# Order of the first loads in a one-core decoder trunk: cache pages ahead of the x tiles, and two more key groups in the opening

## The chip, the cores and the metric

The kernel runs on one core of one Trainium2 chip. The metric is the device time of one execution in microseconds (us), the median over the runs shown. The core has five engines that work side by side and wait for each other by semaphores: TensorE (PE in the profile, its weight loads PEld), VectorE (DVE), ScalarE (ACT), GpSimd (POOL) and SyncE (SP), which here issues nearly all DMAs. On each of them instructions run in the order in which they were queued.

## The reference

The program is one inference step of a two-layer decoder trunk with D = 1024, run for a prompt of 16 meta tokens and 1024 tokens and for 8 samples of 4 new tokens each. Only what this change touches is cut out here:

```
# layer 0, first module
h  = rms_norm(x, norm_mix[0])                  # over all tokens
a, g = split(h @ w_pw1 + b_pw1, 2)
u  = a * sigmoid(g)
y  = causal_dwconv(u, width 31) + b_dw
x  = x + silu(layer_norm(y)) @ w_pw2 + b_pw2
...
# layer 1, sample attention over the paged cache: 8 samples x 16 pages of 128 keys
for phys in page_table:                        # 128 pages in all
    c = cache_kv_latent[phys]                  # (128 keys, 128)
    k = rms_norm(einsum('pc,chd->phd', c, w_uk))   # 16 heads of 64, norm over d
    ...
```

The norm of each cached key does not depend on the tokens. The kernel therefore works out the sums of squares of all 128 x 128 x 16 key vectors during layer 0, long before the attention needs them.

## The kernel before

**Layout.** Activations are kept transposed: 8 tiles x0 to x7 of 128 channels by 1074 token columns (`T0`), 550 KB each. Every float32 operand of a matmul is split into a high part (`ch`, `xh`, `wh`, an ACT copy to fp32r) and a low part (`cl`, `xl`, `wl`, a subtraction on DVE or POOL), and a product is three matmuls: high x high, high x low, low x high. `split` (line 132) does it.

**Key groups.** `cache_norms` (line 634) is a generator that yields 256 times. Each step is one key group: for one page and one half of the 16 heads, three 128x512 matmuls into a PSUM tile `pk` (line 654), an ACT square (line 658, or on some places eight squares with accumulation, line 669) and a sum over each head (a DVE reduction, line 665, in some places after halvings on POOL, line 663). The generator fetches pages four at a time: `fetch(g)` (line 637) loads four latent pages of 128x128 values into one tile `ct` and splits it; `fetch(g + 1)` comes when the third group of page set g is due. There are two `ct`, `ch` and `cl` tiles each and two `pk` tiles.

**Where the groups are called.** `groups(n)` takes the next n steps. The places are fixed numbers: `FIRST0` = 16 ahead of the norm of x and `FIRST` = 30 behind it, both within the opening in which TensorE's order is left to the planner; then 24 for each of the channel blocks c = 1 to 7 (one behind every sixth matmul of the gate gemm of line 419); 12 and 1 and 4 around the last convolution and the layer norm; 8 in the first two column blocks of the `pw2` product (one behind every 18th matmul) and then one behind every ninth matmul, until the 256 are used up. Whatever is taken earlier is missing there: the list runs dry earlier.

**Opening.** `conv_phase` (line 334) loads the key weights `wuk`, the page table `pt` and then the x tiles. `page_table` (line 599) clamps the table on DVE, and `pages` (line 604) lets SP read four page numbers from it into registers and issue one DMA for each page. The SP order in this part is written out by hand: `more(XFIRST)` issues that many tiles of the list x0, ..., x7, `c1` (the constants), and after each page load `between`, a copy of `XPAT`, says how many tiles follow. Before the change this gives:

```
x0 x1 x2 | p0 - p1 x3 p2 - p3 x4 | p4 x5 p5 x6 p6 x7 p7 c1 | weights pw1
```

The sums of squares of x (`sq_add`, line 276: an ACT square and a DVE addition for each tile) lead by `add_rows` (line 295), `rows_rstd` (line 303) and `spread` (line 263) to the norm factor `rstd`. Line 370 scales each x tile with it on DVE, `split` makes `xh` and `xl`, and the first gemm (`gemms`, line 165, matmuls on line 175) of block c = 0 takes them one k after the other. Its two results go through a sigmoid and a product (`glu`, line 397), while TensorE has only key groups to do. Then blocks c = 1 to 7 follow, each with a 31-tap convolution on DVE (line 523) beside the next block's gemm.

**What decides the order.** Instructions on TensorE inside a `manual` block and SP's loads inside `manual_schedule` keep the order of the program. All others are ordered at build time by a planner that simulates the program and prefers higher priorities (`PRIO` = 2000 for the norm of x and for its splits, `PRIO3` = 0 for the first 16 groups).

Of the kernel before, what the change touches and what calls it, by code (L numbers as in the profile page):

```python
# [32 lines left out]
REST = 0  # L33
EVERY2 = 9
EVERY3 = 18
FIRST = 30
FILL0 = 1
FILL2 = 4
NLN = 0
# [21 lines left out]
FILLQ = 4  # L61
ND = 512
FIRST0 = 16
XFIRST = 3
ONPL3 = (1, 3, 5, 7)
PRIO3 = 0
XORD = (0, 1, 2, 3, 4, 5, 6, 7, 8)
XPAT = (0, 1, 0, 1, 1, 1, 1, 1)
ONPL = (0, 2, 4, 6)
ONPL0 = (1, 4, 7)  # L70
PEFILL = (1, 11)
# [47 lines left out]
class Prog:  # L119
# [214 lines left out]
    def conv_phase(self):  # L334
# [3 lines left out]
        with ExitStack() as es:  # L338
# [5 lines left out]
            todo = [(self.c1, a["c1"]) if k == KD else (xs[k], a["x0"][k]) for k in XORD]  # L344
            self.between = list(XPAT)

            def more(n):
                for _ in range(n):
                    nc.sync.dma_start(*todo.pop(0))
            self.more = more  # L350
            with self.tc.manual_schedule(engines={nc.sync.engine}):
                more(XFIRST)
            self.on_dve, self.on_pool = range(8), ONPL3
# [25 lines left out]
            self.on_dve, self.on_pool = range(8), ONPL2  # L379
            self.groups(FIRST)  # L380
            ws = [self.weight(a["pw1"][j * 8], 1024) for j in range(2)]
# [252 lines left out]
    def cache_norms(self):  # L634
        nc, a, kp, ss = self.nc, self.a, self.kp, self.ss

        def fetch(g):
            ct = kp.tile([128, 4, 128], F32, name="ct")
            self.pages(self.pt, 4 * g, [(ct, lambda p: a["ctn"][p].rearrange("a p n -> p (a n)")[:, 0:128])])
            ch, cl = kp.tile([128, 4, 128], F32R, name="ch"), kp.tile([128, 4, 128], F32R, name="cl")  # L640
            self.split(ch, cl, ct, eng=nc.gpsimd if self.help else None)
            return ch, cl

        nxt = fetch(0)
        for g in range(32):
            ch, cl = nxt
            for j in range(4):
                p = 4 * g + j
                for c in range(2):
                    if j == 1 and c == 0 and g < 31:  # L650
                        nxt = fetch(g + 1)
                    ps = self.pk.tile([128, 512], F32, name="pk")
                    for i, (s, m) in enumerate(((ch, self.ukh), (cl, self.ukh), (ch, self.ukl))):
                        x = nc.tensor.matmul(ps, s[:, j, :], m[:, 512 * c:512 * c + 512], start=i == 0, stop=i == 2)  # L654
                    self.pks.append(x)
                    if 2 * j + c in self.on_dve or 2 * j + c in self.on_pool:
                        q = self.ks.tile([128, 512], F32, name="sq")
                        nc.scalar.activation(q, ps, AF.Square)  # L658
                        v, n = q.rearrange("p (a b) -> p a b", b=64), 64
                        while 2 * j + c in self.on_pool and n > self.halve:  # L660
                            n //= 2
                            to = v[:, :, :n] if n > 1 else ss[:, p, 8 * c:8 * c + 8].rearrange("p (a b) -> p a b", b=1)
                            nc.gpsimd.tensor_tensor(out=to, in0=v[:, :, :n], in1=v[:, :, n:2 * n], op=ALU.add)  # L663
                        if n > 1:
                            nc.vector.tensor_reduce(out=ss[:, p, 8 * c:8 * c + 8], in_=v[:, :, :n], op=ALU.add, axis=AX.X)
                    else:
                        for h in range(8):
                            q = kp.tile([128, 64], F32, name="qq")
                            nc.scalar.activation(q, ps[:, 64 * h:64 * h + 64], AF.Square, accum_out=ss[:, p, 8 * c + h:8 * c + h + 1])  # L669
                    yield  # L670
# [1223 lines left out]
```

## Time and profile before

| what | value |
|---|---|
| runs of the kernel before | 2760.22, 2759.51, 2752.87 us, median 2759.51 |
| profiled execution, its own time | 2764.96 us |
| span of its instructions | 2763.0 us |
| busy share of the span | PE 96%, PEld 89%, DVE 68%, ACT 49%, POOL 26% |
| mean granted clock of TensorE | 0.98 |
| moved by DMA | 238.24 MB, mean 86 GB/s |

The profile is of one execution. Its times run from the first instruction; 2.0 us of the execution's own time lie around the span. An engine is busy when an instruction is on it; a matmul's end is modelled, so the distance from one matmul's start to the next says more of its cost than its duration does. "x<-y" is an instruction that writes tile x from y, and a wait is put down to the engine and line that ended it.

### The profile page before, as it was taken

The page shows a single profiled execution, that of the slowest core. Times are in us where ns is not written, and L with a number is a line of the kernel's source. Part 1 is how long each engine was busy: PE and PEld are TensorE (multiplying, and loading weights), DVE is VectorE, ACT ScalarE, POOL GpSimd, SP SyncE. Part 2 cuts the span into 40 slices and gives each one's busy share as a digit, 9 for nine tenths or more (in the row PEclk, how much of TensorE's full clock was granted, in tenths as well). Part 3 has the DMA queues.
Part 4 walks back from the last instruction along what each step waited for, and adds up shares of the span by engine and source line. Part 5 has one row for each costly group of instructions (what it writes and reads, how often), then busy time and mean ns, then how long its engine had stood idle before and what let it go on. Part 6 is the DMA issues. An engine that isn't in the chain of part 4 may idle for free.

```text
span 2763.0 us, 46569 instructions
## 1 busy us (share of the span) xinstructions
PE 2654.5 (96%) x16966; PEld 2449.1 (89%) x16966; DVE 1879.3 (68%) x3485; ACT 1356.8 (49%) x3701; POOL 709.8 (26%) x1019
## 2 busy tenths in 40 slices
PE   7999998999999999999889999999999999999999
PEld 6888876999999999999767776667999999999999
DVE  8899986578888875145677777676378777775232
ACT  6777775345544553023555555576245454453010
POOL 1567663023332330001111212120023333330000
PEclk9999997999999999999889999999999999999999
DMA  4111101502222236132100001367302222226122
GB/s 142 56 41 55 39 28 43 175 30 92 90 92 91 79 120 229 41 95 92 37 10 19 24 24 32 90 202 261 140 24 90 80 80 81 80 96 244 41 87 76
DMA packets 127770, 238.24 MB, mean 86 GB/s; under 512 B 39779, under 2 KB 81141, under 8 KB 127413
## 3 DMA queue, kind: packets, MB, share of 16 engines
q1 hardware_dynamic: 103828, 200.82, 22.4%
q0 software_dynamic: 9600, 32.36, 3.1%
q10 hardware_dynamic: 14112, 2.09, 0.5%
q8 instruction: 133, 2.18, 0.3%
q14 instruction: 97, 0.79, 0.1%
HBM read 183.90 MB, written 51.31 MB: 85 GB/s over the span
## 4 chain that ended last, share of the span: by engine, by line
PE 84%; DVE 6%; ACT 5%; DMA 2%; issue 2%; SPq 0%; POOL 0%; ACTq 0%; DVEq 0%; POOLq 0%
PE ps L797 29%; PE ps L175 22%; PE pk L654 5%; PE g L419 4%; PE v L1339 4%; PE ps L846 3%; PE p L151 2%; PE ps L197 2%; PE ps L1015 1%; PE p L1349 1%; PE p L1351 1%; PE p L1352 1%; PE po L1653 1%; PE s L1309 1%; PE ps L151 1%
## 5 line engine op out<-in xcount | busy, mean ns | idle before, releaser
L135 ACT ACTIVATE wh<-raw 128x512 fp32r<-128x512 f32 (+2 forms) x256 | 191.1, 749 | 539.7 <-PE ps L175 338.2
L136 DVE TENSOR_TENSOR wl<-raw,wh 128x512 fp32r<-128x512 f32 (+2 forms) x244 | 201.5, 829 | 107.4 <-ACT wh L135 105.1
L944 DVE TENSOR_TENSOR x<-ps,x 128x1074 f32<-128x1074 f32 (+1 forms) x48 | 61.0, 1270 | 291.5 <-PE ps L175 291.3
L767 DVE SCALAR_TENSOR_TENSOR c<-ub,c,c 128x1040 f32<-128x1040 f32 (+1 forms) x176 | 225.3, 1312 | 29.5 <-ACT c L763 28.4
L669 ACT ACTIVATE qq<-pk 128x64 f32<-128x64 f32 x736 | 158.4, 244 | 67.8 <-PE pk L654 67.7
L761 POOL COPY sb<-ub 128x32 f32<-128x32 f32 x88 | 87.6, 997 | 393.3 <-DVE ub L808 353.1
L1339 PE MATMUL v<-pf,vf 128*128 128x512 f32 (+4 forms) x448 | 174.4, 473 | 11.1 <-ACT pf L1356 10.7
L663 POOL TENSOR_TENSOR sq<-sq 128x256 f32<-128x256 f32 (+4 forms) x229 | 140.1, 620 | 102.1 <-ACT sq L658 95.1
L1356 ACT ACTIVATE pf<-p 128x512 f32<-128x512 f32 (+4 forms) x224 | 99.1, 450 | 118.0 <-DVE p L1354 97.4
L175 PE MATMUL ps<-xh,wh 128*128 128x358 f32 (+1 forms) x672 | 148.1, 329 | 9.2 <-ACT xh L135 5.9
L669 ACT ACTIVATION_READ_ACCUMULATOR qq<-pk 128x1 f32 x736 | 154.2, 228 | 0.0
L523 DVE SCALAR_TENSOR_TENSOR a<-u,c,a 128x512 f32<-128x512 f32 x216 | 150.2, 747 | 4.9 <-ACT a L516 4.9
L175 PE MATMUL ps<-xl,wh 128*128 128x358 f32 (+1 forms) x672 | 147.8, 328 | 0.1
L175 PE MATMUL ps<-xh,wl 128*128 128x358 f32 (+1 forms) x672 | 147.3, 327 | 0.0
L175 PE MATMUL ps<-al,wh 128*128 128x358 f32 (+1 forms) x672 | 147.2, 327 | 0.0
L175 PE MATMUL ps<-ah,wl 128*128 128x358 f32 (+1 forms) x672 | 146.5, 326 | 0.0
L175 PE MATMUL ps<-ah,wh 128*128 128x358 f32 (+1 forms) x672 | 146.2, 326 | 0.0
L654 PE MATMUL pk<-ukh,ch 128*128 128x512 f32 x256 | 115.3, 451 | 26.1 <-ACT ch L135 13.6
L763 ACT ACTIVATE c<-ub,c 128x1074 f32<-128x1074 f32 (+1 forms) x88 | 101.5, 1187 | 60.0 <-DVE ub L808 46.3
L175 PEld LDWEIGHTS ps<-xh,wh 128*128 128x128 f32 x672 | 117.2, 191 | 12.8 <-ACT xh L135 6.8
L658 ACT ACTIVATE sq<-pk 128x512 f32<-128x512 f32 x164 | 99.8, 613 | 50.3 <-PE pk L654 47.5
L135 ACT ACTIVATE wh<-s 128x512 fp32r<-128x512 f32 x120 | 75.6, 630 | 93.5 <-PE ps L797 86.7
(599 smaller groups left out, 9111.5 us busy)
## 6 DMA issues: line engine op xcount, KB each, us to landing
raw<-wup SPq DMA_DIRECT2D x88, 512.0 KB, 3.6
pg<-ctn SPq DMA_DIRECT2D x128, 192.0 KB, 3.8
raw<-wdn SPq DMA_DIRECT2D x32, 448.0 KB, 3.4
raw<-pw SPq DMA_DIRECT2D x24, 512.0 KB, 3.9
d_a<-c POOLq DMA_DIRECT2D x22, 537.0 KB, 3.5
raw<-d_a SPq DMA_DIRECT2D x22, 537.0 KB, 5.1
d_a<-c POOLq DMA_DIRECT2D x22, 531.0 KB, 3.2
raw<-d_a SPq DMA_DIRECT2D x22, 531.0 KB, 5.3
```

Source lines behind the costliest of these rows:

```text
L135: return (nc.scalar.activation(h, src, AF.Copy), (eng or nc.vector).tensor_tensor(out=l, in0=src, in1=h.bitcast(F32), op=ALU.subtract))
L136: (eng or nc.vector).tensor_tensor(out=l, in0=src, in1=h.bitcast(F32), op=ALU.subtract))
L175: nc.tensor.matmul(p[:, c, :ch], s[:, k * 128:(k + 1) * 128], m[k][:, off + c * ch:off + (c + 1) * ch], start=k == 0 and i == 0, stop=k == ...
L419: y = nc.tensor.matmul(p[:, 0], x[:, k * 128:(k + 1) * 128], m[k][:, t * ch:t * ch + ch], start=k == 0 and i == 0, stop=k == KD - 1 and i ...
L523: nc.vector.scalar_tensor_tensor(out=p[:, :ND] if j == n - 1 else acc, in0=x[:, j:j + ND], scalar=w[:, j:j + 1], in1=to if j == 1 else acc ...
L654: x = nc.tensor.matmul(ps, s[:, j, :], m[:, 512 * c:512 * c + 512], start=i == 0, stop=i == 2)
L663: nc.gpsimd.tensor_tensor(out=to, in0=v[:, :, :n], in1=v[:, :, n:2 * n], op=ALU.add)
L669: nc.scalar.activation(q, ps[:, 64 * h:64 * h + 64], AF.Square, accum_out=ss[:, p, 8 * c + h:8 * c + h + 1])
L763: x = nc.scalar.activation(c, ub, AF.Copy, scale=wd[:, t, 2:3])
L767: nc.vector.scalar_tensor_tensor(out=c[:, 2:pe], in0=ub[:, tap:tap + pe - 2], scalar=wd[:, t, tap:tap + 1], in1=c[:, 2:pe], op0=ALU.mult, ...
L797: nc.tensor.matmul(ps, w[:, s], m[:, lo:hi], start=first and k == 0 and i == 0, stop=k == KD // 2 - 1 and i == 2, skip_group_check=True)
L1339: nc.tensor.matmul(o[:, at_:], vf[:m, b, c], p[:m, :512 - at_], start=b == 0, stop=last)
```

## The change

Three numbers and one branch change. `XFIRST` goes from 3 to 0 and `XPAT` from (0, 1, 0, 1, 1, 1, 1, 1) to (0, 0, 0, 3, 1, 2, 1, 2), so the SP order becomes:

```
p0 p1 p2 p3 x0 x1 x2 | p4 x3 p5 x4 x5 p6 x6 p7 x7 c1 | weights pw1
```

In `fetch(0)` the tile is split page by page: four copies and four subtractions of 128x128 in place of one each of 128x512. All later fetches are split as before. `FIRST` goes from 30 to 32, so 48 key groups lie in the opening in place of 46, and each later place gets groups that stand two further on in the list.

```diff
-FIRST = 30
+FIRST = 32
...
-XFIRST = 3
+XFIRST = 0
...
-XPAT = (0, 1, 0, 1, 1, 1, 1, 1)
+XPAT = (0, 0, 0, 3, 1, 2, 1, 2)
...
             ch, cl = kp.tile([128, 4, 128], F32R, name="ch"), kp.tile([128, 4, 128], F32R, name="cl")
-            self.split(ch, cl, ct, eng=nc.gpsimd if self.help else None)
+            if g:
+                self.split(ch, cl, ct, eng=nc.gpsimd if self.help else None)
+            else:
+                for j in range(4):
+                    self.split(ch[:, j], cl[:, j], ct[:, j])
             return ch, cl
```

## Rows read from the trace of the kernel before

**Rows 1.** Page: busy shares of the engines and the granted clock in 40 slices.

```profile
PE 2654.5 (96%) x16966; PEld 2449.1 (89%) x16966; DVE 1879.3 (68%) x3485; ACT 1356.8 (49%) x3701; POOL 709.8 (26%) x1019
...
PEclk9999997999999999999889999999999999999999
```

**Rows 2.** Page: the chain that ended last, by engine.

```profile
PE 84%; DVE 6%; ACT 5%; DMA 2%; issue 2%; SPq 0%; POOL 0%; ACTq 0%; DVEq 0%; POOLq 0%
```

**Rows 3.** Windows: stretch and length, busy of each engine, clock, DMA share, GB/s.

```profile
core 0: us, PE busy (x) PEld busy (x) DVE busy (x) ACT busy (x) POOL busy (x), PEclk, DMA share, GB/s
0.00:13.60 13.60, 0.01 (x1) 0.01 (x1) 4.71 (x6) 7.25 (x7) 0.20 (x4) 1.00 0.85 294
13.60:22.60 9.00, 7.86 (x16) 4.79 (x17) 7.72 (x11) 7.17 (x10) 1.64 (x3) 1.00 0.99 372
22.60:47.00 24.40, 22.97 (x103) 15.81 (x103) 24.23 (x46) 19.69 (x35) 10.98 (x15) 1.00 0.28 83
47.00:80.00 33.00, 33.00 (x185) 31.18 (x184) 28.43 (x34) 17.16 (x26) 0.70 (x7) 1.00 0.08 20
...
440.00:460.00 20.00, 10.51 (x39) 8.76 (x40) 11.90 (x22) 9.83 (x12) 0.59 (x4) 0.51 0.00 0
...
5.00:6.00 1.00, 0.00 (x0) 0.00 (x0) 0.22 (x1) 0.32 (x1) 0.00 (x0) 1.00 0.99 403
...
22.00:23.00 1.00, 0.88 (x3) 0.68 (x3) 1.00 (x2) 1.00 (x3) 0.74 (x1) 1.00 0.48 142
```

**Rows 4.** Waits of TensorE from 13 to 85 us: total, times, longest.

```profile
PE pk L654 <- ACT ch L135: 13.6, 1, 13.6
```

**Rows 5.** Timeline, 0 to 24 us: start, us, instruction, idle before.

```profile
5.37 0.22 DVE L602 TENSOR_SCALAR pt<-pt 1x128 int32<-1x128 int32 x1 [4.36 <-DMA pt<-pt]
...
6.35 0.88 SPq L613 DMA_DIRECT2D ct<-ctn  x2
...
7.05 1.10 ACT L279 ACTIVATE sq<-x 128x1074 f32<-128x1074 f32 x1 [0.30 <-DMA x<-x]
...
12.92 0.61 ACT L135 ACTIVATE ch<-ct 128x512 fp32r<-128x512 f32 x1
...
14.24 0.69 DVE L136 TENSOR_TENSOR cl<-ct,ch 128x512 fp32r<-128x512 f32 x1
...
20.09 1.09 ACT L282 ACTIVATE q<-x 128x1074 f32<-128x1074 f32 x1
20.21 0.63 PE L654 MATMUL pk<-ukl,ch 128*128 128x512 f32 x1
...
20.63 0.63 PE L654 MATMUL pk<-ukh,ch 128*128 128x512 f32 x1
...
21.65 0.27 DVE L377 TENSOR_TENSOR wsum<-c 128x120 f32<-128x120 f32 x1
...
21.92 1.26 DVE L283 TENSOR_TENSOR sq<-sq,q 128x1074 f32<-128x1074 f32 x1
```

**Rows 6.** The page tile `ct`, 0 to 30 us: its loads from issue to landing.

```profile
DMA to landing us min/median/max: 1.8/4.1/6.0
```

**Rows 7.** Page: the group of small ACT squares, count, busy, mean ns.

```profile
L669 ACT ACTIVATE qq<-pk 128x64 f32<-128x64 f32 x736 | 158.4, 244 | 67.8 <-PE pk L654 67.7
```

**Rows 8.** Groups by line and form, 13.6 to 85 us: busy, mean ns.

```profile
L665 DVE TENSOR_REDUCE ss<-sq 128x8 f32<-128x512 f32 x35 | 22.8, 676 | 4.0 <-ACT sq L658 4.0
...
L665 DVE TENSOR_REDUCE ss<-sq 128x8 f32<-128x128 f32 x8 | 2.2, 272 | 0.0
```

**Rows 9.** The chain of waits where the key groups run dry.

```profile
522.49 1.38 PE pk L654 x6
523.86 22.20 PE ps L175 x135
```

**Rows 10.** Waits of TensorE from 85 to 420 us: total, times, longest.

```profile
PE pk L654 <- ACT sq L658: 7.3, 9, 2.3
PE pk L654 <- ACT qq L669: 3.0, 2, 1.5
```

## The prediction

> **What bounds the kernel.** I read the page first. TensorE is busy 96% of the span and no other engine over 68%, apart from TensorE's own weight loads [rows 1], and 84% of the chain that ended last is TensorE's own work [rows 2]. So a change in the opening can win only what TensorE now idles or crawls there, and a place that loses a key group wins its TensorE time. Next I read windows. TensorE does nothing for 13.6 us, is busy 7.86 of the next 9.0, 22.97 of the next 24.4 and all 33.0 after that [rows 3]. The waits say what ends the empty start: the high part `ch` of the first page tile [rows 4]. The timeline shows why so late: the page loads could first be issued at 6.35 us, after the table had been clamped at 5.37, and the one split of all four pages ran at 12.92, since the four loads are interleaved with x tiles in one queue [rows 5]. DVE is the second thing to watch: busy 24.23 of 24.4 us from 22.6 on [rows 3].
>
> The first matmuls are also slow. Near 20 us two of them start 0.42 us apart [rows 5], where two whole groups of three late in layer 0 take 1.38 us, 0.23 each [rows 9]. That is 512 columns at 1.2 and at 2.4 GHz. The granted-clock column says 1.00 for both stretches [rows 3], so here I go by the distances. A group costs 1.28 us at the lower level and 0.69 at the higher; in the kernel before the change comes near 22.6 us.
>
> **Part 1: pages in front.** The first page load still waits for the table, so I leave its issue at 6.35 us. Its landing is bounded by this tile's fastest and median loads, 1.8 and 4.1 us [rows 6]. I take 1.8, because the queue ahead then holds only the key weights and two small state loads. That gives 8.15. The split of one page has no row: on ACT it lies between a 128x64 square, 0.24 us [rows 7], and the 128x512 copy, 0.61 [rows 5]; I take 0.30, in proportion to the columns. On DVE the nearest row is 128x120 at 0.27, the upper bound the 128x512 at 0.69 [rows 5]; I take 0.28. The first matmul needs only `ch`, so TensorE starts near 8.6 us, 5.0 earlier than now (2.7 if the median landing holds: 6.35 + 4.1 + 0.3 = 10.8). Four pieces cost 4 x 0.30 - 0.61 = 0.6 us more on ACT (bounds 0.4 and 1.8) and 4 x 0.28 - 0.69 = 0.4 more on DVE (bounds 0.4 and 2.1). Both engines then wait for x tiles, which cover it; without that cover the DVE part counts in full, below.
>
> **Part 2: x tiles behind.** The DMA engines are full (share 0.99 at 5 to 6 us) until 22 to 23 us, where the share falls to 0.48 [rows 3]. About 6.8 MB go through (eight x tiles of 0.55, weights, pages, constants), near 0.39 MB/us. Now x0 to x2 no longer start ahead of the table wait, so the engines have little to do from about 5 to 8 us. At the same rate four pages and eight x tiles with the next four pages, 4.9 MB, end near 8.0 + 12.6 = 20.6 us. The last x tile's square runs at 20.09 today and the last addition of squares ends at 23.18 [rows 5]; 20.6 + 1.1 + 1.3 gives 23.0. The norm of x is therefore about level: the first square moves from 7.05 [rows 5] to about 10.5, but the end of this chain was held by DVE and ACT as much as by the loads. Bounds: nothing, and the full 3 us by which the stream starts later. The weights of the first gemm land 2 us later and are needed only behind the norm.
>
> **Part 3: how far the early start carries.** The second four pages now stand behind seven x tiles: 0.5 + 3.85 MB, so they land near 19 us, and with one 0.6 us split that may queue behind a 1.1 us square, TensorE has more to eat at about 20.5. The eight groups of the first four pages need at most 8 x 1.28 = 10.3 us, until 19. So at 20.5 eight groups are done at either clock. From there to 22.6 come 1.6 groups at the lower clock or 3.0 at the higher, together 9.6 to 11. The kernel before has 16 matmul starts by 22.6 [rows 3], 5.3 groups. The lead is 4.3 to 5.7 groups, at 0.69 that is 3.0 to 3.9 us of TensorE.
>
> DVE has its own lead: by 23 us it has done the reductions of about five groups more, some at 0.68 and some at 0.27 us [rows 8], about 2.4, less the 0.4 of part 1: 2.0 us.
>
> **Part 4: two more groups.** In the opening they cost TensorE 1.4 us and DVE two reductions, 1.35. What remains at the end of the first gemm is 3.45 - 1.4 = 2.0 us by TensorE and 2.0 - 1.35 = 0.65 by DVE, which was as full as TensorE up to 47 us and has slack behind it (28.43 of 33.0) [rows 3]. I take 1.5. Bounds: 2.5 earlier (3.9 less 1.4), or, if the full 3 us of part 2 reach the gemm, 1.5 later. In the `pw2` product the list runs dry two groups sooner. There TensorE goes on without a break into 135 matmuls [rows 9], so the two groups' 1.38 us come off in full.
>
> **The sum.** 1.5 + 1.4 = 2.9 us: span 2763.0 to 2760.1, profiled execution 2764.96 to 2762.1. The shown median, 2759.51, lies 5.45 below that profiled execution; minus 2.9 it is 2756.6 us. From the bounds, -3.9 to +0.1: 2755.6 to 2759.6. The shown runs of one kernel spread over 7.35 us, so 0.3% (8.3 us) is about what a measurement can tell from no change.
>
> **A rule weighed.** In the layer norm TensorE is busy 10.51 of 20 us and its granted clock is 0.51 [rows 3]: with gaps it falls to the lower level. The Trainium skill, TensorE: Matmul & The Clock Gate, section "HAM oscillation — how this bites in real kernels", says that a matmul burst which then waits for its next load can fall back and start the next burst slow. By it, the early start could buy eight groups and then lose the clock at the seam near 19 us. No row of the kernel before has this seam. By this rule the sum is that of the second rival; by the rows of part 3 it is the forecast's.
>
> **The rivals.**
>
> *No net gain: the norm of x is late.* If `rstd` is later by the whole 3 us, the x tiles are scaled later on a full DVE and the early groups only fill the wait. The gemm ends 1.5 us later, the `pw2` end gives 1.4 back: 2759.6 us. For it: DVE is full from 22.6 to 47 [rows 3]. Against: the sum of part 2 ends level.
>
> *Clock lost at the seam.* TensorE pauses from 19 to 20.5 us and then runs at the lower level for as long as it did the first time, 9.0 us (13.6 to 22.6). It stays at half rate until 29.5, 6.9 us longer than now, which costs 3.45 us of work. The end of the gemm is 2.0 - 3.45 = 1.5 later, and the total again about the old one, 2759.6. The rule weighed above is on this side. Against it: the clock rose in those 9 us in spite of 1.14 us of idle [rows 3].
>
> *Slower: the groups' places in the convolution blocks.* Blocks 1 to 7 have 21 column blocks with eight groups each, and every eighth group is now two places earlier in them: the fetch and its split meet another part of the sigmoid, taps and weight splits. If each column block waits 0.6 us more for ACT on `pk`, that is 12.6 us: 2756.6 + 12.6 = 2769.2. It decides from 0.14 us a block (2.9 / 21). For it: today such waits are 7.3 + 3.0 us in all [rows 10], and they hang on this order. Against: odd and even groups keep their parity, so the long ACT groups stay where they are.
>
> *Clearly faster.* The same shift could remove most of those 10.3 us. If 7 go, 2756.6 - 7 = 2749.6. The same evidence speaks for and against it, and it gains from any half-rate stretch that goes with a wait.
>
> *It does not do what it says:* if the planner queues the page splits behind x squares, TensorE starts at 10 to 11 us. By the 2.7 us bound that still leaves eight groups by 20.5 or 21, so the result moves by under a microsecond; it is inside the forecast.
>
> **Chances and range.** Forecast, 1 to 5 us faster: 0.48. Norm late or clock lost, within 2 us of before: 0.18. Slower by the places: 0.12, of it 0.08 beyond 0.3%. Faster by the places: 0.22, nearly all beyond 0.3%, since 2751.2 is the bound. So faster 0.22, same 0.70, slower 0.08. The range holds the first two, with the run spread about them, most of the faster case and half of the slower: 2746 to 2766; the likeliest case's own range is 2753 to 2760.
>
> **What would show it.** Right: the first key-group matmul at 8 to 9 us (11 at most); 24 of them before any with the second page set, and that set near 20; the last x square ending near 21.5 to 22; the first gemm's last matmul about 1.5 us before 80; the last key group followed by about six matmuls' worth more of the `pw2` run. Wrong: 0.42 us distances still seen past 23 us (clock), the first scaling of x by line 370 more than 1 us past its place before (norm late), or `pk` waits from 85 to 420 us far from 10.3 us (places). A result beyond 8 us either way must come from the last of these, not from the opening, which has only 13.6 us of empty start and some 5 us of slow clock to give.

## The result, and the profile after

The changed kernel takes 2768.94 us (median of 10 runs, 2762.66 to 2775.01); the kernel before, run beside it, 2757.99 us (10 runs, 2752.87 to 2760.57). The ratio is 1.0040, 95% interval 1.0030 to 1.0049: 11 us slower, where 2.9 us faster was forecast. It lies outside the range of 2746 to 2766, beyond the 0.3% bound on the side that had a chance of 0.08. The profiled execution took 2770.57 us, with a span of 2768.7.

The page after: busy time of the engines, then the granted clock in 40 slices, to set beside [rows 1].

```profile
PE 2649.9 (96%) x16966; PEld 2446.6 (88%) x16966; DVE 1880.8 (68%) x3488; ACT 1356.6 (49%) x3704; POOL 709.7 (26%) x1019
...
PEclk9999997999999999999989999999999999999999
```

Nothing here tells where 11 us went: TensorE does the same 16966 matmuls, and its busy time is even 4.6 us less. The span is longer by waits and not by work, so the loss has to be looked for by stage. First the opening, windows of the changed kernel (columns as in [rows 3]), then the waits of TensorE from 8 to 85 us (total, times, longest), then its timeline.

```profile
0.00:8.50 8.50, 0.03 (x1) 0.03 (x1) 2.17 (x4) 3.71 (x4) 0.20 (x4) 1.00 0.51 170
8.50:19.00 10.50, 8.03 (x18) 5.41 (x19) 5.89 (x11) 6.85 (x12) 2.37 (x3) 1.00 0.96 346
19.00:22.60 3.60, 2.02 (x8) 1.02 (x6) 2.00 (x3) 3.60 (x6) 3.07 (x5) 1.00 1.03 406
22.60:47.00 24.40, 19.05 (x83) 13.44 (x84) 23.72 (x45) 17.87 (x31) 8.02 (x11) 0.93 0.36 111
47.00:83.00 36.00, 35.49 (x195) 32.92 (x194) 31.32 (x37) 19.62 (x29) 0.80 (x8) 1.00 0.08 22
```

```profile
PE pk L658 <- ACT ch L135: 13.3, 2, 8.5
PE pk L658 <- ACT sq L662: 3.3, 3, 2.5
```

```profile
2.52 0.36 SPq L156 DMA_DIRECT2D raw<-pw  x1
5.34 0.22 DVE L602 TENSOR_SCALAR pt<-pt 1x128 int32<-1x128 int32 x1 [4.33 <-DMA pt<-pt]
...
6.32 1.90 SPq L613 DMA_DIRECT2D ct<-ctn  x4
...
8.11 0.31 ACT L135 ACTIVATE ch<-ct 128x128 fp32r<-128x128 f32 x1 [0.20 <-DMA ct<-ctn]
8.27 1.37 SPq L349 DMA_DIRECT2D x<-x  x3
...
8.47 1.22 PE L658 MATMUL pk<-ukh,ch 128*128 128x512 f32 x2 [8.47 <-ACT ch L135]
...
10.87 0.63 PE L658 MATMUL pk<-ukl,ch 128*128 128x512 f32 x1
...
12.34 1.10 ACT L279 ACTIVATE sq<-x 128x1074 f32<-128x1074 f32 x1 [1.66 <-DMA x<-x]
...
13.34 1.07 ACT L662 ACTIVATE sq<-pk 128x512 f32<-128x512 f32 x2
...
13.97 0.79 PE L658 MATMUL pk<-ukh,ch 128*128 128x512 f32 x1 [2.48 <-ACT sq L662]
...
20.91 0.39 PE L658 MATMUL pk<-ukl,ch 128*128 128x512 f32 x1
...
24.47 1.10 ACT L282 ACTIVATE q<-x 128x1074 f32<-128x1074 f32 x1 [1.23 <-DVE sq L283]
...
25.47 0.61 ACT L135 ACTIVATE ch<-ct 128x512 fp32r<-128x512 f32 x1
...
26.14 1.22 PE L658 MATMUL pk<-ukh,ch 128*128 128x512 f32 x2 [4.84 <-ACT ch L135]
26.25 1.10 ACT L282 ACTIVATE q<-x 128x1074 f32<-128x1074 f32 x1 [0.16 <-DVE sq L283]
...
28.39 1.27 DVE L283 TENSOR_TENSOR sq<-sq,q 128x1074 f32<-128x1074 f32 x1
```

TensorE starts at 8.47 us, as forecast. It then stops twice. After the matmul at 10.87 both `pk` tiles are full, and their squares (13.34) stand in ACT's queue behind the square of x0, which waits for its DMA until 12.34. After the matmul at 20.91 it has eaten the first four pages; the second four are split at 25.47, behind squares of x which themselves wait for DVE's additions (1.23 us at 24.47). One load stands elsewhere than in the order given under *The change*: the first 512 KB of `pw1` weights left SP's queue at 2.52 us, ahead of the pages, and not behind everything. The starts in this trace add up like this: 22 key-group matmuls by 20.5 us against 12 in the kernel before, 24 against 22 by 26 us, 33 against 36 by 30 us. The whole lead is gone at 30 us.

The second place is the last convolution. TensorE's waits from 85 to 420 us in the changed kernel; [rows 10] has those of before, with a `fb` wait of 2.5 us that is not among its rows:

```profile
PE pk L658 <- ACT sq L662: 12.5, 21, 1.8
PE g L532 <- DVE fb L509: 7.5, 1, 7.5
...
PE pk L658 <- ACT qq L673: 0.8, 1, 0.8
```

**A ledger.** To add this up I took, for each kernel, the start of the same TensorE matmul at several points, less its start in the profile of before (us; plus is later). "Sums" is the first matmul of line 300, "c1" the first of line 419, "c1, 2nd" the 49th, "c7 end" the last one, "conv" the first of line 532 (line numbers of before), "latents" one in layer 1 near 1300 us, before the attention. The last columns are the ratio to before from runs on one chip and its interval.

```
kernel                 first pk  sums    c1   c1,2nd  c7 end  conv  latents   ratio
changed                  -5.1    +6.0   +3.1   +5.5    +3.9   +8.9   +11.0    1.0040 [1.0030, 1.0049]
 1 groups only           +0.5    -0.7   +0.3   +2.6    +0.9   +5.9    +7.9    1.0019 [1.0010, 1.0029]
 2 loads only            -5.0    +6.3   +5.9   +5.9    +5.2   +5.2    +5.4    1.0013 [1.0002, 1.0024]
 3 order only            -3.0    +4.8   +2.5   +3.5    +1.9   +1.9   +10.0    1.0028 [1.0015, 1.0040]
 4 page split only       -2.0    -1.0   -0.1   -0.8    -2.2   +0.8    +2.7    1.0014 [1.0001, 1.0026]
 5 places moved          -5.0    +4.7   +3.5  +13.1   +11.3  +11.3   +11.1    1.0052 [1.0034, 1.0069]
 6 changed, fb first     -5.2    +5.9   +3.0   +5.4    +3.7   +6.2    +7.0    1.0030 [1.0019, 1.0041]
 7 groups, fb first      +0.2    -1.1   -0.1   +2.3    +0.5   +2.8    +5.6    1.0027 [1.0016, 1.0038]
 8 loads, no seams       -5.0    +5.5   +5.5   +4.8    +3.7   +6.9    +8.7    1.0021 [1.0009, 1.0034]
 9 3 groups ahead        -5.3    +4.5   +3.2   +1.7    -0.3   -0.3    -0.2    1.0029 [1.0014, 1.0044]
10 squares of x first    -5.3    +3.5   +2.0   +6.9    +7.1   +7.1   +10.7    1.0034 [1.0024, 1.0045]
11 one x ahead           -3.8    +5.3   +4.3   +3.8    +1.6   +4.6    +5.6    1.0018 [1.0007, 1.0029]
12 three x ahead         -2.4    +0.1   +1.0   +0.3    -1.9   +1.1    +2.2    1.0012 [1.0001, 1.0022]
13 x on ACT's queue      +0.9    +5.6   +3.4   +5.2    +5.2   +8.2   +10.2    1.0034 [1.0022, 1.0046]
14 three x, fb first     -1.7    +0.3   +2.0   +1.3    -0.8   -0.3    +7.5    1.0018 [1.0009, 1.0028]
15 split, fb first       -1.6    -0.6   +0.4   -0.4    -2.3   -1.7    -1.2    0.9993 [0.9982, 1.0004]
16 the same again        -1.5    -0.8   +0.2   -0.5    -2.6   -2.1    -2.0    0.9997 [0.9987, 1.0007]
17 before, fb first      +0.4    -0.8   +0.2   +0.2    +0.1   +0.1    +3.8    1.0010 [1.0000, 1.0021]
```

Runs 15 and 16 are one kernel profiled twice; they agree within 0.8 us up to the latents, and are 6.9 us apart at 2000 us, behind the attention. So the ledger is read up to there; a time's median is the judge of the whole. For the changed kernel the ledger's +11.0 and the median's +10.95 agree, in part by luck: the two profiled executions end 5.7 us apart (spans 2763.0 and 2768.7). For the other runs the two figures lie within some 3 us of each other, but not for run 9 (level at the latents, 8 us slower by the median). Its profiled execution, 2753.75 us, is the fastest of its eight, whose median is 2765.57; so its row does not stand for the run.

**TensorE's account before c1.** Kernel before and changed kernel both run 132 key-group matmuls (44 groups) and 144 gemm matmuls before c1. Counting 0.231 us for one of 512 columns, 0.163 for one of 358 and 0.11 for the small ones (the distances of undisturbed starts), that is 56.9 us of work. What the distances hold beyond that I put down to the lower level where two starts are 0.40 to 0.46 us apart, and to stops elsewhere. In us, before and after 30 us of the span:

```
                      first pk  work   stops to 30  lower level to 30  stops later  lower later   c1 at
before                  13.6    56.9       4.3             2.0            5.7          0.0         82.5
changed                  8.5    56.9      10.7             3.1            6.2          0.2         85.6
2 loads only             8.6    56.9      11.3             2.7            7.2          1.6         88.4
8 loads, no seams        8.6    58.3      10.5             2.3            6.1          2.2         88.0
10 squares of x first    8.3    53.5      12.7             2.7            4.9          2.3         84.5
 4 page split only      11.6    58.3       6.3             1.4            4.4          0.4         82.4
12 three x ahead        11.1    58.3       6.1             2.0            5.6          0.4         83.5
```

The 5.2 us won at the start are lost again, and 3.1 more with them: 6.4 us more of stops and 1.1 more at the lower level before 30 us, and 0.7 later. Run 10 has less work in its row because fewer key groups were done by c1, and those with 58.3 have two more groups done.

### The profile page after: what moved, and what is told of

It is laid out like the page before. It is cut to its first block, busy times and chain, and to the rows that moved or that the text cites. A ratio compares the mean times of both kernels' runs of the same rounds, so it can differ in the third digit from the quotient of the medians.

```text
span 2768.7 us, 46590 instructions
## 1 busy us (share of the span) xinstructions
PE 2649.9 (96%) x16966; PEld 2446.6 (88%) x16966; DVE 1880.8 (68%) x3488; ACT 1356.6 (49%) x3704; POOL 709.7 (26%) x1019
## 4 chain that ended last, share of the span: by engine, by line
PE 83%; ACT 6%; DVE 6%; DMA 2%; issue 2%; POOL 1%; SPq 1%; ACTq 0%; DVEq 0%; POOLq 0%
PE ps L801 30%; PE ps L175 22%; PE pk L658 5%; PE v L1343 4%; PE ps L850 3%; PE g L419 3%; PE p L151 2%; PE ps L197 2%; ACT qq L673 1%; PE ps L1019 1%; PE p L1353 1%; PE p L1356 1%; PE p L1355 1%; PE s L1313 1%; PE ps L151 1%
## 5 line engine op out<-in xcount | busy, mean ns | idle before, releaser
L1343 PE MATMUL v<-pf,vf 128*128 128x512 f32 (+4 forms) x448 | 176.8, 478 | 10.6 <-ACT pf L1360 10.3
```

The source lines that it names most:

```text
L1343: nc.tensor.matmul(o[:, at_:], vf[:m, b, c], p[:m, :512 - at_], start=b == 0, stop=last)
```

## The experiments

**Runs 1 and 2: the change in two halves.** Run 1 is the kernel before with the first edit below, run 2 the changed kernel with the second.

```diff
-FIRST = 30
+FIRST = 32
...
-FIRST = 32
+FIRST = 30
```

> The kernel before with 32 key groups in place of 30 and nothing else. Places theory (the list position of the groups, 48 in place of 46, puts a page fetch and its split in front of the last convolution, and there costs about 5 us): start of the last convolution's TensorE part about 5 us late against the blocks before it, its wait for the tile fb near 7.5 us in place of 2.5; opening about 1.4 us longer for two groups, pw2 product 1.4 us shorter; total 4 to 6 us above before. Opening theory (the whole loss comes from the new load order): total within 1 us of before.

> The changed kernel with 30 key groups, so the new load order and the page-wise split alone. Places theory: wait for fb in the last convolution back to about 2.5 us; the opening still ends late, by the 3.1 us of the changed kernel less 1.4 us for the two groups, about 1.7 us; total 1 to 4 us above before. Opening theory: total about 11 us above before, as the changed kernel.

Both halves are slower. The loads alone are 5.9 us late at c1, where 1.7 had been expected, and stay 5.2 to 5.9 late. The groups alone cost nothing before c1 (+0.3), 2.4 in its first column block, because 36 key-group matmuls lie there instead of 30 (1.4 us) and a wait for ACT's squares grows from 0.4 to 1.4 us; blocks c1 to c7 give 1.7 back, and 5.0 are lost at the last convolution, with the `fb` wait of 7.5 us that was expected. At c1 the halves do not add up: +0.3 and +5.9 alone, +3.1 together, with the same 132 key-group matmuls done. Most of the 2.8 us between run 2 and the changed kernel lie after 30 us (by the account 1.4 at the lower level and 1.0 in stops). Why is open.

**Run 5: the places shifted by eight.** The changed kernel with this edit: 54 groups in the opening, eight more than 46, so that each block meets the groups that it met before, one page set on.

```diff
-FIRST = 32
+FIRST = 38
```

> The changed kernel with 38 key groups in place of 32: 54 in the opening, so every later place gets groups at the same point of their page set as in the kernel before (54 and 46 leave the same rest by 8). Places theory: wait for fb back to about 2.5 us, opening about 4.1 us longer than in the changed kernel, pw2 product about 4.1 us shorter; total about 5 us below the changed kernel, 5 to 7 above before. Opening theory: total as the changed kernel, 11 above before, or more.

The `fb` wait at the last convolution is back at 2.5 us and nothing is lost there (c7 end and conv both +11.3). But eight more groups don't fit behind the norm: they spill into the first column block of c1 (+9.6 us there). The total, expected some 5 us below the changed kernel, is 2769.89 us and therefore says nothing for or against the places; the step at the last convolution does.

**Runs 6 and 7: the bias's place.** In the last convolution `fb`, line 509's sum that TensorE waits for, is made to stand ahead of the second tap in DVE's queue; run 6 in the changed kernel, run 7 in run 1.

```diff
-                nc.vector.scalar_tensor_tensor(out=p[:, :ND] if j == n - 1 else acc, in0=x[:, j:j + ND], scalar=w[:, j:j + 1],
+                t = nc.vector.scalar_tensor_tensor(out=p[:, :ND] if j == n - 1 else acc, in0=x[:, j:j + ND], scalar=w[:, j:j + 1],
                                                in1=to if j == 1 else acc, op0=ALU.mult, op1=ALU.add)
+                if diag and j == 1:
+                    self.follow(t, [first])
```

> The changed kernel with one order added: in the last convolution the first tap on VectorE may not be queued ahead of the instruction that makes fb. Groups and loads stay as changed. If the loss there is the five taps queued ahead of fb (the places theory's mechanism), the wait for fb falls from 7.5 us by 3 to 5 us and the total by 3 to 5 us against the changed kernel, to 6 to 8 above before. If the taps only fill a time in which something else is late, the total stays 11 above before.

> The kernel before with 32 key groups, and fb ahead of the first taps in the last convolution. Places theory: the wait for fb falls by about 2.5 us as it did with the new loads, total about 3 us below the kernel with 32 groups alone, 2 to 3 above before. If the rest of the loss with 32 groups lies in the blocks or behind, it stays 4 to 5 above before.

(In these texts the word bias stands for `fb`; it is the sum of the even and odd columns of u.) The step from c7 end to conv falls from 5.0 to 2.5 us in run 6 and from 5.0 to 2.3 in run 7. The times don't show it: run 6 has 1.0030 against the changed kernel's 1.0040, and run 7 has 1.0027 against 1.0019 in run 1, and in both pairs the intervals overlap. The traces show why half remains. First GpSimd and VectorE of the kernel before, then of the changed kernel, then one line of run 6:

```profile
391.29 1.26 POOL L663 TENSOR_TENSOR sq<-sq 128x256 f32<-128x256 f32 x2
393.25 0.21 POOL L435 COPY us<-u 128x30 f32<-128x30 f32 x1 [0.70 <-DVE u L403]
...
393.77 0.72 DVE L509 TENSOR_TENSOR fb<-u 128x535 f32<-128x535 f32 x1
395.44 1.42 DVE L523 SCALAR_TENSOR_TENSOR a<-u,c,a 128x512 f32<-128x512 f32 x2 [0.95 <-ACT a L516]
```

```profile
395.51 1.64 POOL L136 TENSOR_TENSOR cl<-ct,ch 128x512 fp32r<-128x512 f32 x1 [0.42 <-ACT ch L135]
397.11 2.44 POOL L446 TENSOR_TENSOR total<-total,x 128x1074 f32<-128x1074 f32 x1
399.50 0.20 POOL L435 COPY us<-u 128x30 f32<-128x30 f32 x1
...
396.32 0.84 DVE L403 SCALAR_TENSOR_TENSOR u<-g,c,sg 128x358 f32<-128x358 f32 x1 [0.30 <-ACT sg L402]
399.41 3.40 DVE L523 SCALAR_TENSOR_TENSOR a<-u,c,a 128x512 f32<-128x512 f32 x5 [2.25 <-ACT a L516]
402.14 0.06 DVE L437 MEMSET u<- 128x1 f32 x1
402.71 0.71 DVE L509 TENSOR_TENSOR fb<-u 128x535 f32<-128x535 f32 x1
```

```profile
399.86 0.06 DVE L437 MEMSET u<- 128x1 f32 x1 [2.92 <-POOL us L436]
```

`u` is complete near 397.2, but the copies of it that must precede the memset of its last column stand in POOL's queue behind a page split (`cl`) and an addition; and DVE has taps queued ahead of memset and `fb`. The edit takes away the second delay and leaves the first: in run 6 the memset comes at 399.86, as soon as POOL's copies are done. Two groups more put a page split into just this stretch.

**Run 8: no seams.** Run 2, and in addition the square of x0 stands behind the first two key-group squares, and that of x6 behind the split of the second four pages.

```diff
+            self.follow(y, self.sqs.pop("two", []))
...
+        if k == 6:
+            self.follow(y, self.sqs.pop("ch", []))
```

> New loads with 30 key groups, and two orders added on ScalarE: the first x square behind the first two key-group squares, the square of x6 behind the split of the second four pages. That takes away two stops of TensorE (2.8 us near 11 us and 5.2 us near 21 us), and hardly moves the norm of x. Seam theory (the opening loses its time because TensorE stands still there and comes back at the lower clock): the conv blocks start 3 to 5 us sooner than with the new loads alone, which were 5.9 us behind the kernel before. Norm theory (the norm's chain starts with the landing of x0 and is paced by VectorE and ScalarE, so the gemm waits for it whatever TensorE did): the conv blocks start within 1 us of where they did with the new loads alone.

c1 comes at +5.5 instead of +5.9, and I first read this as the late norm winning over the seams. TensorE's account corrects that reading: the two long stops became four shorter ones of 1.0 to 2.7 us, and the stops to 30 us are 10.5 instead of 11.3. The order on ACT was changed, the sum of the stops hardly. One thing stays on the side of the late norm: by 30 us run 8 had started 36 key-group matmuls, as many as the kernel before, and c1 still came 5.5 us late, with two more groups done (1.4 us).

**Runs 9 and 10: who slows the sums over x.** Run 9 is the changed kernel with the first two edits; run 10 adds the third, by which the squares of the key groups 4 to 24 follow the last square of x on ACT.

```diff
-FIRST = 32
+FIRST = 43
...
-FIRST0 = 16
+FIRST0 = 3
...
-                        nc.scalar.activation(q, ps, AF.Square)
+                        y = nc.scalar.activation(q, ps, AF.Square)
+                        if 3 <= 8 * g + 2 * j + c < 24:
+                            self.follow(y, self.xlast)
```

> The changed loads with only 3 of the key groups in front of the norm (43 behind it, 46 in all, where the kernel before has 16 and 30). If the key groups' squares and reductions between the squares of x set the pace of the sums (17.3 us from the first square to the last add in the changed kernel), that stretch falls to 10 to 12 us, and the sums come near 24 us even though the first x tile lands at 12 us. If the loads of x or the adds themselves set it, the stretch stays over 15 us. The 13 groups moved behind the norm cost about 0.46 us of matmuls each (up to 6 us) in the gemm stretch or in c1, so the total is no better than +3 us by either.

> As the run with 3 key groups in front of the norm, and in addition ScalarE takes the squares of the key groups 4 to 24 only after the last square of x. In that run ScalarE was busy for 15.5 of the 17.0 us of the stretch and had 12 or so key squares in it, since the planner had pulled groups from behind the norm into it; so it did not test what it was meant to. If a full ScalarE, with key squares between the squares of x, is what makes the sums take 17 us from the first x tile, the sums come 3 to 6 us sooner than in that run (28.5 us), at 22 to 25 us. If the landing of the x tiles or VectorE's adds (1.27 us each) set the pace, they stay at 27 us or later. The total says little here: TensorE loses its groups of that stretch and they are done later; c1 starts 2 to 6 us later than before by either.

Run 9 tested nothing of this: the planner drew later groups into the stretch, and it still took 17.0 us from the first square of x (11.45) to the end of the last addition (28.41). In run 10 it took 14.1, the timeline of x there:

```profile
12.26 1.10 ACT L279 ACTIVATE sq<-x 128x1074 f32<-128x1074 f32 x1 [2.24 <-DMA x<-x]
...
17.53 6.80 DVE L283 TENSOR_TENSOR sq<-sq,q 128x1074 f32<-128x1074 f32 x5
...
25.11 1.27 DVE L283 TENSOR_TENSOR sq<-sq,q 128x1074 f32<-128x1074 f32 x1
```

So the key squares account for some 3 of the 17 us; the rest is the eight tiles themselves, five additions at 1.36 us apiece. The loads would not have let it be much shorter: x3 to x7 landed 1.4 to 1.6 us apart, the last at 22.52, 0.6 us ahead of its square. The sums came at 27.5, one us sooner than in run 9: the second expectation, with a share of the first. And this is the run in which the norm is earliest among those with pages in front, yet TensorE stops longest (12.7 us to 30) and has 15 key-group matmuls fewer done at c1 than the kernel before. An earlier norm does not pay when ACT's key squares are its price.

**Runs 11 and 12: x tiles ahead again.** Run 2 with one x tile in front of the pages (run 11, the first two added lines), and with three (run 12, the last two).

```diff
-XFIRST = 0
-XPAT = (0, 0, 0, 3, 1, 2, 1, 2)
+XFIRST = 1
+XPAT = (0, 0, 0, 2, 1, 2, 1, 2)
...
+XFIRST = 3
+XPAT = (0, 0, 0, 2, 1, 1, 1, 1)
```

> The changed opening with 30 groups, but one x tile stays ahead of the page table and the pages, where the kernel before has three and the changed one none. If the lateness of the norm comes from the wait for the first x tile, its square begins near 7.0 us again and the sums over x come near 24 + 1 us (with no x tile ahead +6.3, with three +0.1); c1 then starts 1 to 3 us later than before. If the later x tiles and the key groups between set the pace whatever comes first, the sums stay 4 us or more late and c1 starts 4 to 5.5 us late. TensorE starts 3 to 5 us earlier than before in either case. Total: +1 to +3 us by the first, +4 to +6 by the second.

> 30 key groups, the page-wise split kept, loads in the order x0 x1 x2, four pages, x3 x4, then page and x tile in turn: the x chain starts as in the kernel before, the first page set comes in one piece behind three x tiles. Norm theory: sums of x ready within 1 us of the kernel before, first key-group matmul near 10 us in place of 13.6, conv blocks start 0 to 2 us earlier than before, total 0 to 2 below before. Seam theory: the second page set is as late as in the changed kernel, so TensorE stops near 20 us again and the conv blocks start 2 us or more late.

One tile is not enough: x0's square runs at 6.86, the next waits for its tile until 13.26, and the sums stay 5.3 us late. Three tiles bring the sums level (+0.1) with TensorE still 2.4 us earlier, and c1 comes 1.0 us later with two groups more done (1.4 us). c7 then ends 1.9 us earlier than before; the last convolution takes 3.0 of it, with a `fb` wait of 5.5 us although 46 groups lie in the opening. The time is above before (1.0012), where 0 to 2 us below had been expected. So the number of groups is not what brings the late `fb`; each arrangement of the queues has its own.

**Run 13: x tiles from ACT's queue.** Run 2 with x0 to x2 issued at 0.74 us by ACT, SP free for the page table, and the splits of `wuk` and the clamp ahead of the first squares and additions of x.

```diff
-            with self.tc.manual_schedule(engines={nc.sync.engine}):
-                more(XFIRST)
+            for _ in range(3):
+                nc.scalar.dma_start(*todo.pop(0))
...
-XPAT = (0, 0, 0, 3, 1, 2, 1, 2)
+XPAT = (0, 0, 0, 1, 1, 1, 1, 2)
```

Its timeline, then the split of the key weights in the kernel before:

```profile
0.74 1.38 ACTq L355 DMA_DIRECT2D x<-x  x3
...
1.70 0.44 SPq L630 DMA_DIRECT2D raw<-wuk  x1
2.19 0.52 SPq L604 DMA_DIRECT2D pt<-pt  x1
...
9.24 0.21 DVE L605 TENSOR_SCALAR pt<-pt 1x128 int32<-1x128 int32 x1 [8.23 <-DMA pt<-pt]
9.24 1.06 ACT L135 ACTIVATE ukh<-raw 128x1024 fp32r<-128x1024 f32 x1 [5.81 <-DMA raw<-wuk]
10.21 1.91 SPq L616 DMA_DIRECT2D ct<-ctn  x4
```

```profile
5.68 1.06 ACT L135 ACTIVATE ukh<-raw 128x1024 fp32r<-128x1024 f32 x1 [3.66 <-DMA raw<-wuk]
```

> 30 key groups; x0 to x2 issued from ScalarE's DMA queue at the start, four pages first on SyncE's, so that neither waits for the other's issue; the planner is held to clamp the page table and split the key weights first. Norm theory: sums of x ready within 1 us of the kernel before, first key-group matmul at 9 to 11 us, conv blocks start 1 to 3 us earlier than before, total 1 to 3 below before. If the pages' landing behind three x tiles in the same DMA engines is what counts, the first matmul comes near 12 us and the total is as before.

It has neither. The 0.5 KB page table is in use only at 9.24 instead of 5.37 [rows 5], so the pages go out at 10.21, and TensorE starts 0.9 us later than before. The 512 KB of key weights, which stand right ahead of the table in SP's own queue, are late by as much: their split starts at 9.24 instead of 5.68. So the three tiles on ACT's queue held up SP's loads as a whole. Whether the table waited for the tiles or for the weights ahead of it was not tried.

**Runs 3 and 4: order and split apart.** Run 3 is the kernel before with the first part of this alone, run 4 with the second alone.

```diff
-XFIRST = 3
-XPAT = (0, 1, 0, 1, 1, 1, 1, 1)
+XFIRST = 0
+XPAT = (0, 0, 0, 3, 1, 2, 1, 2)
...
-            self.split(ch, cl, ct, eng=nc.gpsimd if self.help else None)
+            if g:
+                self.split(ch, cl, ct, eng=nc.gpsimd if self.help else None)
+            else:
+                for j in range(4):
+                    self.split(ch[:, j], cl[:, j], ct[:, j])
```

> The kernel before with the new order of the loads alone: page table and pages ahead of the x tiles, the first four pages split in two whole pieces as before, 30 groups. If the order alone makes the norm late, its sums come 5 to 6.5 us later than before and c1 starts 4.5 to 6 us later, as with order and page-wise split together (+6.3 and +5.9), while TensorE starts 3 to 4.5 us earlier. If the page-wise split has a part in it, the sums come less than 4.5 us late. Total: +2 to +5 us by the first, 0 to +3 by the second.

> The kernel before with one part of the change alone: the first four pages split page by page; the order of the loads (three x tiles first, its old pattern) and the 30 groups as before. If the page-wise split is harmless and useful by itself, TensorE starts 0.5 to 2 us earlier, the sums over x stay within 0.5 us, and the total is -1 to +1 us. If eight small pieces in place of two large ones take ScalarE and VectorE from the squares of x, the sums come 1 us or more late and c1 starts 0.5 us or more late.

The order alone makes the sums 4.8 us late and c1 2.5 (with one pair of groups fewer done by then, 126 matmuls). Less than I had expected, so neither bound was met at c1. The page split alone is a gain up to the end of c7: TensorE 2.0 us earlier, sums 1.0 earlier, two more groups before c1 at the same time, and c7 ends 2.2 us earlier. Then the last convolution takes 3.0 by a late `fb` (5.5 us again), and by its time the run is slower than before (1.0014). Run 3's loss behind the convolution, 6 us, is another queue on DVE: TensorE waits 3.6 us for `x` of line 541 (0.2 before), and the granted clock of the stretch from 400 to 470 us is 0.73 in place of 0.78.

**Runs 14 to 17: keeping that gain.** Run 14 is run 12, runs 15 and 16 run 4, and run 17 the kernel before, each with the diff shown for runs 6 and 7.

> Three x tiles ahead, page-wise split, 30 groups (1.9 us earlier than before at the end of c7, then 3.0 us lost at the start of the last convolution behind a bias `fb` that came 5.5 us late), now with the first two taps' order fixed, so that the bias is ahead of the second tap in VectorE's queue. If the place of the bias in VectorE's queue is the cause, the loss falls from 3.0 to near 0.5 us, and the total lies 0 to 2 us under the kernel before. If the cause is GpSimd's queue (the adds and copies ahead of the memset that the bias waits for), the loss stays near 3 us and the total 1 to 3 us over it.

> The kernel before with the page-wise split of the first four pages (2.2 us earlier than before at the end of c7, then 3.0 us lost behind the late bias `fb`), and in the last convolution the bias ahead of the second tap in VectorE's queue. If the bias's place is all that eats the gain, the last convolution starts 1.5 to 2.2 us earlier than before, and that holds up to the latents: total -1 to -2.2 us, the first version below the kernel before. If another wait takes its place (with three x tiles ahead and the same edit, the final combination of the convolution came late for its sums and 5.5 us went there), the latents are level with before or up to 5 us late, and the total is 0 to +4 us.

> The kernel with the page-wise split and the bias ahead of the second tap once more, in more rounds: 0.9993 [0.9982, 1.0004] before, with the profile's marks 1.2 to 2.3 us ahead of the kernel before from the end of c7 to the latents. If that lead reaches the end, the ratio is 0.9992 to 0.9996 with an interval that ends below 1; if the attention stages take it back, 0.9997 to 1.0003.

> The kernel before with the bias's place alone. There the bias already stood ahead of all taps (bias 393.8, first tap 395.4 us). If the lead of the kernel with both edits comes from the page-wise split, this one is level with the kernel before up to the latents (within 0.5 us). If the edit of the place carries it, its marks are 1 us or more ahead from the last convolution on and level ahead of it.

Run 14 starts the last convolution 0.3 us early, but its end on DVE comes late (3.2 us of TensorE waiting for `x`), and 5.5 us go there. Run 15 keeps 1.7 us at the start of the last convolution and 1.2 to the latents, its repetition 2.1 and 2.0. In time that is 0.9993 and 0.9997, both intervals across 1: no difference that was measured, and the only version with a part of the change that is not slower. Run 17 is level with before (+0.1 to +0.6 from c1 on) up to the closing of layer 0's first module, so the lead of 15 and 16 comes from the split. Then it loses 2.9 us by 700 us, although its engines have the instructions of the kernel before in the same order there; windows of run 17, then of before, then one of the changed kernel:

```profile
540.00:575.00 35.00, 34.06 (x207) 33.72 (x206) 13.12 (x27) 5.71 (x9) 0.30 (x3) 0.95 0.31 103
575.00:630.00 55.00, 52.74 (x411) 52.09 (x410) 47.86 (x85) 28.51 (x56) 21.48 (x10) 0.97 0.06 21
```

```profile
540.00:575.00 35.00, 33.15 (x208) 32.59 (x207) 13.94 (x28) 6.96 (x11) 0.30 (x3) 1.00 0.29 99
575.00:630.00 55.00, 53.65 (x432) 53.22 (x433) 49.10 (x86) 30.54 (x60) 23.69 (x17) 1.00 0.08 25
```

```profile
575.00:630.00 55.00, 51.80 (x390) 50.90 (x391) 46.91 (x92) 25.48 (x48) 14.94 (x4) 0.97 0.08 31
```

The granted clock is 0.95 and 0.97 where before it is 1.00 in both. The changed kernel has 0.97 in the second, 3% of the clock over 55 us, or some 1.6 us; this accounts for the +1.5 that its ledger gains between the closing and the first ffn.

## Why the prediction was wrong

**Part 1 held.** First page 1.79 us from issue to split (taken: 1.8), pieces of 0.31 on ACT and 0.29 on DVE (0.30 and 0.28), first matmul at 8.47 (8.6). That the first `pw1` weights also went ahead of the pages (2.52) did not hold them up.

**Part 3 is the step that failed in the opening.** It let the eight groups of the first four pages run through and the second four pages arrive for TensorE at 20.5 us, with 3.0 to 3.9 us of lead left at 22.6. The last matmul of the eight groups started at 20.9, close to that. But the second pages' `ch` ran at 25.47. The part set their landing near 19 and let one square stand ahead of them. Their last page went out at 15.44, between x6, which landed at 21.44, and x7 (22.92), so by an estimate from these two it was there near 21.6; and ACT then had squares of x to do first, held by DVE's additions, for another 4 us. The part also had no stop inside the eight groups, where TensorE stood for 2.5 us behind the square of x0. Now ACT works for both, the norm and the key groups, and x comes to it later: it was busy 4.64 us of the first 12 instead of 5.72, and 19.4 of the first 30 instead of 20.2 (DVE 17.4 instead of 19.8). With the two stops and the lower level after them the opening gained nothing and lost 3.1 us at c1, where 1.5 had been forecast as gain, at worst a loss of 1.5. That ACT's queue is the cause is read from the waits; run 8, which changed only its order, left c1 nearly where it was.

**Part 2 was wrong too.** It set the norm by the end of the loads, "about level", at most 3 us late. The sum let the load stream run at its full rate from 8.0 us, without the time from a load's issue to its landing: x0, issued at 8.27, was there only at 12.3, and x7 at 22.92 instead of 20.6. The first square of x came at 12.34 instead of the 10.5 taken there, and from it to the last addition it took 17.3 us, against 16.1 before [rows 5], 14.1 to 17.2 in runs 3, 4, 9, 10, 12 and 15, and 18.2 in run 13. So the sums follow the first tile's landing, with one tile ahead the second's (run 11), and a chain of much the same length; in the changed kernel the last tile's landing (22.92) did not set them, since its square ran at 26.25. So the sums came 6.0 us late. What that by itself costs is not known: run 10 had earlier sums and longer stops.

**Part 4 left out the other half.** The 1.4 us of the `pw2` product came off (1.5 by the ledger). But the forecast put what the two groups do between the opening and `pw2` at nothing. They cost nothing before c1, then 2.4 us in its first column block (run 1: 1.4 of matmuls and 1.0 of wait) and 5.0 us at the last convolution, by a page split and taps that now stand ahead of `fb` (run 1 has the 5.0 with the old loads, run 2 nothing with the new ones).

**The rivals.** *Norm late* and *clock lost at the seam* both named a true thing and were too small. The seam came, later and longer than supposed, and the starts behind it are 0.42 to 0.52 us apart from 27.16 to 29.03 and then 0.23, so the lower level lasted some 3 us and not 9; the granted clock of 0.93 over 22.6 to 47 us says the same. That is the case in the Trainium skill, TensorE: Matmul & The Clock Gate, section "HAM oscillation — how this bites in real kernels", of a burst that starts slow after a wait for its data. The trace agrees; the price before 30 us is 1.1 us here, against 6.4 for the stops themselves. *Slower by the places* gave 2769.2, and 2768.94 was measured, but that is a coincidence, since its mechanism did not come. It set 0.6 us on each of 21 column blocks of c1 to c7; the blocks behind the first one together are 1.6 us faster, though the `pk` waits are 13.3 us in place of 10.3. What the places did cost, besides c1's first column block, is one event, 5.0 us at the last convolution, which no rival had. *Clearly faster* and *It does not do what it says* did not come (first matmul at 8.47). The prediction also held that a result beyond 8 us must come from the places and not from the opening; here 3.1 us are the opening's and 7.4 the places' (2.4 and 5.0).

The sum for the changed kernel up to the first ffn, from the ledger: opening +3.1, c1's first column block +2.4, the rest of c1 to c7 -1.6, last convolution +5.0 and +0.6 to its end, layer norm to `pw2` +0.6, `pw2` -1.5, then +1.5 in a piece at the lower clock: +10.1, where the median says +10.95.

**Open.** Which of the late norm and the stops sets c1 was not separated: run 8 kept the late norm and only broke the stops up, and run 10 made the norm earlier and the stops longer. The late `fb` was mended by half; that the rest comes from its copies in POOL's queue is read from the trace, and moving them ahead was not tried.

## What to carry to other kernels

An engine that is started earlier gains only what its suppliers can keep up: count, up to the next stage, its work, its stops and its slow stretches, and look for the queue that feeds it as well as the waiting chain (here ACT, which served both). A chain that begins with the first tile and then takes much the same time in every version is set by when the first tiles land, so these are the last that should be moved back. And a planner's order far behind an edit can cost more than the edit itself: take a ledger of fixed marks through the whole kernel, and test the parts of a change one by one: here one of three, the page-wise split, won 2 us up to the end of c7, and none made the kernel measurably faster.

## What the runs showed of the hardware

Loads issued on one queue hold up those of another. When ACT had issued 1.65 MB of x at 0.74 us (run 13), the 512 KB of key weights on SP's queue, issued at 1.70, were in use at 9.24 instead of 5.68, and the 0.5 KB page table behind them at 9.24 instead of 5.37. A small load that others depend on is then late too. I don't say which part of the path holds it.

The granted clock of TensorE is not the same in two executions of the same work. Run 17 has the order of the kernel before and is at 0.95 and 0.97 where that is at 1.00 (540 to 630 us), which costs 2.9 us. Runs 15 and 16 are one kernel: from 1800 to 1940 us they are at 0.91 and 0.98, and there most of the 6.9 us arise that part them at 2000 us. A mark in one profile carries some 3 us of this before 1300 us, which is as much as most edits here, and more behind.
